# Attention scores: the products with the keys' low parts contract over 64 rows, both halves of the keys side by side in the array

## The chip, the cores and the metric

The kernel runs on one core of a Trainium2 chip. Its time is the device time of one execution in microseconds (us); three runs of the kernel before gave 2217.49, 2220.78 and 2222.54 us, so the time before is their median, 2220.78 us. A difference of 0.2% of that is 4.4 us.

The engines have the names that the profile gives them: PE is the matrix engine (PEld is its load of weights, the operand that stays in the array while the other streams through), DVE the vector engine, ACT the scalar engine, POOL the general engine, SP the one that issues the transfers. PSUM is the memory that matrix products are written to, in banks of 128 rows by 512 floats.

## The reference, cut to what matters

Two layers over 1024 tokens of width 1024. In each layer, one projection of the normalised input feeds three mixers, of which the attention is the one that the change touches:

```python
q = _axial_rope(_rmsnorm(q.reshape(b, s, 8, 64), q_norm_g[l]), tabs)   # 8 query heads of 64
k = _axial_rope(_rmsnorm(k.reshape(b, s, 2, 64), k_norm_g[l]), tabs)   # 2 key heads, 4 query heads each
...
sc = jnp.einsum('bqgrd,bkgd->bgrqk', qblk, k).astype(jnp.float32) * 64 ** -0.5
p = jax.nn.softmax(sc, axis=-1)
return jnp.einsum('bgrqk,bkgd->bqgrd', p, v)
```

A query block has 128 queries, and every query sees all 1024 keys. All arrays are float32. After the mixers come an output projection and a gated convolutional MLP.

## The kernel before, in words

**Numbers in two parts.** The fast matrix product here takes operands of the type `float32r`, which hold fewer digits than float32. To keep the digits, an operand x is split into a high part h (x rounded to `float32r`) and a low part l = x - h, and a product of two split operands is the sum of several matrix products into the same bank. Elsewhere in the kernel a product costs three of them (`mm3`, lines 130 to 132: high by high, high by low, low by high).

**The scores.** A head has 64 channels and the array has 128 rows, so the attention stacks the two parts of the queries: `q_transpose` (line 584) transposes the queries of a block on PE into a bank, ACT copies them, rounded, into rows 0 to 63 of the tile `qT` (line 598), and DVE writes the low parts into rows 64 to 127 (line 599); it does so for the even heads (e = 0) and the odd heads (e = 1) apart. `kv_block` (line 540) writes each key's channels twice, one copy below the other, so that the high parts of the keys lie in all 128 rows, and likewise the low parts. One pass over 128 rows with the keys' high parts then gives (query high + query low) times key high, and a second pass with the keys' low parts gives (query high + query low) times key low. `att_scores` (line 608) makes the scores of 128 queries and one head against 1024 keys in four products, each 128 rows by 512 keys: high and low for the first 512 keys into one bank (lines 616 and 617), then the same for the last 512 keys into the next bank. The keys are in four tiles, one for each key head and half of the keys, in the slots E9, W1, W4 and W5. Each of these groups of four is followed by a maximum over the 1024 scores on DVE (line 619), an exponential on ACT (line 622), a reciprocal on DVE (624) and a scaling on POOL (625).

**The order of the work.** `attention` (line 666) runs units: one unit is a query block and a key head, 16 units in each layer, each with four score groups. A unit has eight steps kc. In step kc, PE transposes the probabilities of the unit before, 128 keys of them (`att_T`, line 633; ACT copies them out at line 637, DVE writes the low parts at line 638), makes a score group of its own unit where kc is 0, 1, 3 or 4, makes some products of the convolution's projections as filler (line 301), and multiplies by the values with a lag of two steps (lines 645 and 646). In step 5 of every second unit `q_transpose` prepares the next query block. PE's order is the order in which this is written, since the stage is under manual order for PE; the other engines' orders are set by a scheduler. Scores go to two pairs of banks (`big`), transposed probabilities to two banks (`pa`), taken in turns.

There are 16 units of four groups in each of two layers, 128 score groups and 512 score products in all.

Of the kernel before, what the change touches and what calls it, by code (L numbers as in the profile page):

```python
# [9 lines left out]
F32R = mybir.dt.float32r  # L10
AF = mybir.ActivationFunctionType
# [3 lines left out]
P = 128  # L15
# [41 lines left out]
class Trunk:  # L57
# [26 lines left out]

    def S(self, tag, shape=(1024,), dt=F32):
        return self.slot(tag, shape, dt)
# [47 lines left out]
    def wpiece(self, src, raw, h, l, eh="p", el="p"):  # L134

        sh = list(src.shape[1:])
        w = self.S(raw, sh)
        self.nc.sync.dma_start(w, src)
        th, tl = self.S(h, sh, F32R), self.S(l, sh, F32R)
        self.split(th, tl, w, eh, el)  # L140
# [3 lines left out]
    def consts(self, L):  # L144
        nc, i = self.nc, self.i
        raw = self.S("W4", [2, P])
        nc.gpsimd.memset(raw, 0.0)
# [37 lines left out]
    def ropetabs(self):  # L185
        nc = self.nc
        cs = self.S("W4", [2, 8, 64])
        nc.sync.dma_start(cs[:, 0], self.i["cos_tab"].rearrange("(b p) c -> p b c", p=P))
# [39 lines left out]
    def spread_g(self, rows, tag):  # L228
# [6 lines left out]
        self.warm(WARM[1])  # L235
        gb = self.S("G6", [KC, P])
        t = self.slot(tag, [D])
# [302 lines left out]
    def kv_block(self, b, hT):  # L540
        nc = self.nc
        if b % 4 == 0:
            for g in range(2):
                self.kT[g][b // 4] = self.S(("E9", "W1", "W4", "W5")[2 * g + b // 4], [2, 512], F32R)
            self.V[b // 4] = self.S(("E3", "E4")[b // 4], [4, 2, 2, 64], F32R)
        acc = self.acc("pa")
        self.tok_mm(acc[:, 0:256], hT, b, self.kvw, 4)
        av = acc[:, 128:256].rearrange("p (g c) -> p g c", c=64)
        V = self.V[b // 4]
        nc.scalar.activation(V[:, b % 4, :, 0, :], av, AF.Copy)  # L550
        nc.vector.tensor_tensor(
            out=V[:, b % 4, :, 1, :], in0=av, in1=V[:, b % 4, :, 0, :].bitcast(F32),
            op=ALU.subtract,
        )
        kr = self.small("kr", [P, 128], bufs=2)
        if b == 0:
            self.ktmp = self.S("E5", [4, 2, 128])
        tmp = self.ktmp[:, b % 4]
        self.rope(kr, acc, 2, self.ktab, b, tmp)
        if b == 0:  # L560
            self.kcat = self.S("E0", [2, 2, 2, 2, 64], F32R)
        kc = self.kcat[:, b % 2]
        k3 = kr.rearrange("p (g c) -> p g c", c=64)
        kb = k3.unsqueeze(2).to_broadcast([P, 2, 2, 64])
        self.split(kc[:, :, 0], kc[:, :, 1], kb, "a", "v")
        pt = self.acc(("po", "pf")[b % 2], dt=F32R)
        kf = kc.rearrange("p g l d c -> p (g l) (d c)")
        for j in range(4):
            nc.tensor.transpose(pt[:, j * P : (j + 1) * P], kf[:, j, :], self.identr)
        for g in range(2):  # L570
            nc.scalar.activation(
                self.kT[g][b // 4][:, :, (b % 4) * P : (b % 4 + 1) * P],
                pt[:, g * 256 : g * 256 + 256].rearrange("p (l t) -> p l t", l=2), AF.Copy,
            )

    def q_block(self, b, hT):
        if b % 2 == 0:
# [5 lines left out]

    def q_transpose(self, b):

        nc = self.nc
        q = self.q[b // 2][:, b % 2, :]
        pt = self.big()[:, 0:512]
        for j in range(4):
            nc.tensor.transpose(  # L590
                pt[:, j * P : (j + 1) * P], q[:, j * P : (j + 1) * P], self.ident
            )
        pv = pt.rearrange("p (j t) -> p j t", j=4)
        qT = self.S("G0", [4, 2, P], F32R)
        for e in range(2):
            src = pv[64 * e : 64 * e + 64]
            h = qT[0:64, :, e, :]
            nc.scalar.activation(h, src, AF.Copy)
            nc.vector.tensor_tensor(
                out=qT[64:128, :, e, :], in0=src, in1=h.bitcast(F32), op=ALU.subtract  # L600
            )
        self.qT = qT.rearrange("p j e t -> p (j e) t")

    def ring(self):
        self.phn += 1
        return f"E{6 + self.phn % 3}"

    def att_scores(self, u, r, pu):

        nc = self.nc  # L610
        g = u % 2
        S = self.big()
        for half in range(2):
            o = S[:, half * 512 : half * 512 + 512]
            q = self.qT[:, 4 * g + r, :]
            nc.tensor.matmul(o, q, self.kT[g][half][:, 0, :], start=True, stop=False)  # L616
            nc.tensor.matmul(o, q, self.kT[g][half][:, 1, :], start=False, stop=True)  # L617
        nm = self.small("nm", [P, 1], bufs=4)
        nc.vector.tensor_reduce(out=nm, in_=S, op=ALU.max, axis=AX.X, negate=True)  # L619
        sm = self.small("sm", [P, 1], bufs=4)  # L620
        p = pu[:, r, :]
        nc.scalar.activation(p, S, AF.Exp, bias=nm, accum_out=sm)  # L622
        rv = self.small("rv", [P, 1], bufs=4)
        nc.vector.reciprocal(rv, sm)  # L624
        nc.gpsimd.tensor_scalar(  # L625
            out=p, in0=p, scalar1=rv, scalar2=1.0, op0=ALU.mult, op1=ALU.mult
        )
# [537 lines left out]
    def run(self, depth):  # L1165
        nc, i = self.nc, self.i
# [5 lines left out]
        for L in range(depth):  # L1172
# [1 line left out]
                self.alloc_x(self.xreg)  # L1174
            self.su, self.vnh, self.vnl = [0, 0], [0, 0], [0, 0]
            self.mB, self.mA = [0, 0], [[0, 0], [0, 0]]
            self.kT, self.V, self.q = [[0, 0], [0, 0]], [0, 0], [0] * 4
            self.phn = self.wun = 0
            if L == 0:
                hT, xs = self.begin(xin)  # L1180
# [189 lines left out]
```

## Time and profile before

| | |
|---|---|
| median of three runs | 2220.78 us (2217.49 to 2222.54) |
| the profiled execution | 2218.71 us, its span 2216.7 us |
| PE busy | 2199.8 us, 99% of the span |
| PEld busy | 1828.3 us, 82% |
| DVE busy | 1505.1 us, 68% |
| ACT busy | 1110.0 us, 50% |
| POOL busy | 1102.5 us, 50% |
| score products | the first starts at 143.8 us, the last at 1456.9 us |
| granted clock of PE | 1.00 |

The attention of the first layer holds the stretch from 155 to 368 us, that of the second the stretch from 1258 to 1471 us.

Times inside the profile count from the first instruction of the profiled execution. In a view by groups, a row gives the line, the engine, the operation, what it writes and reads, the shape, how many there were, their summed and mean durations, and how long the engine had idled just before them. In a timeline a row gives the start and the duration of one instruction, or of several alike that follow each other (the count at the end). A matrix product's row ends later than the next one's row starts, because products are pipelined: what a product costs in a stream is the distance between two starts, not its duration.

### The profile page before, as it was taken

Reading aid. Unit: us, or ns where it says so; the run is one execution under the profiler, and the core shown is the slowest. Engines: PE = TensorE matmul, PEld = TensorE weight load, DVE = VectorE, ACT = ScalarE, POOL = GpSimd, SP = SyncE. Lnnn points to the kernel's source line nnn. Section 1 sums busy time; section 2 is a strip of 40 time slices with the busy share of each in tenths; the row PEclk is TensorE's granted clock in tenths of the full one; section 3 lists DMA queues with packets and bytes.
Section 4 is the critical chain, followed back from the end, with each engine's and each line's share of the span. In section 5 each row is a group of like instructions: output and inputs, shape, how many; then the busy total and the mean of one; then the engine's idle time right before and its main releaser. Section 6 shows DMA issues by size and latency. Waiting matters only on the chain.

```text
span 2216.7 us, 29437 instructions
## 1 busy us (share of the span) xinstructions
PE 2199.8 (99%) x10590; PEld 1828.3 (82%) x10590; DVE 1505.1 (68%) x1973; ACT 1110.0 (50%) x1890; POOL 1102.5 (50%) x1031
## 2 busy tenths in 40 slices
PE   9999999999999999999999999999999999999999
PEld 7888888887888888888888888888788888888887
DVE  6568887177777777754745688862867777777554
ACT  5247776364444444433532477763545444544332
POOL 4364445576767776020133653556667767751100
PEclk9999999999999999999999999999999999999999
DMA  5000002223545453886520000041234545448754
GB/s 178 26 20 10 11 19 96 105 83 98 166 157 168 154 168 123 296 314 216 200 91 11 20 20 1 29 154 47 76 124 152 171 152 167 156 143 326 283 190 164
DMA packets 202020, 281.91 MB, mean 127 GB/s; under 512 B 15598, under 2 KB 121618, under 8 KB 201874
## 3 DMA queue, kind: packets, MB, share of 16 engines
q1 hardware_dynamic: 201874, 280.03, 37.6%
q8 instruction: 83, 1.36, 0.3%
q14 instruction: 63, 0.52, 0.1%
HBM read 199.77 MB, written 80.22 MB: 126 GB/s over the span
## 4 chain that ended last, share of the span: by engine, by line
PE 92%; DVE 2%; POOL 2%; ACT 1%; DMA 1%; issue 1%; SPq 0%; DVEq 0%; POOLq 0%; ACTq 0%
PE pa L890 20%; PE pf L890 9%; PE big L1114 8%; PE pa L1114 5%; PE pa L633 5%; PE pf L301 5%; PE po L890 5%; PE pf L1114 3%; PE po L1114 3%; PE big L616 3%; PE po L645 3%; PE big L617 3%; PE po L646 3%; PE pa L132 2%; PE pa L131 2%; PE pa L130 2%
## 5 line engine op out<-in xcount | busy, mean ns | idle before, releaser
L625 POOL TENSOR_SCALAR H<-H,rv 128x1024 f32<-128x1024 f32 x128 | 144.1, 1127 | 223.3 <-DVE rv L624 223.3
L106 ACT ACTIVATE E<-E 128x512 fp32r<-128x512 f32 (+1 forms) x211 | 133.0, 637 | 162.3 <-POOL E L878 61.0
L638 DVE TENSOR_TENSOR E<-pa,E 128x512 fp32r<-128x512 f32 x256 | 173.5, 688 | 52.2 <-ACT E L637 50.6
L890 PE MATMUL pa<-H,E 128*128 128x512 f32 x840 | 206.6, 390 | 1.4 <-DVE H L936 1.3
L637 ACT ACTIVATE E<-pa 128x512 fp32r<-128x512 f32 x256 | 152.8, 597 | 80.0 <-PE pa L633 78.4
L117 POOL TENSOR_TENSOR E<-E,E 128x512 fp32r<-128x512 f32 x118 | 165.1, 1404 | 50.8 <-ACT E L106 50.8
L890 PEld LDWEIGHTS pa<-H,E 128*128 128x128 f32 x840 | 157.4, 188 | 35.3 <-DVE H L936 2.1
L106 ACT ACTIVATE G<-H 128x1024 fp32r<-128x1024 f32 (+1 forms) x116 | 114.2, 1008 | 142.3 <-PE big L1114 70.8
L117 DVE TENSOR_TENSOR G<-H,G 128x1024 fp32r<-128x1024 f32 (+1 forms) x86 | 99.5, 1160 | 110.8 <-ACT G L106 110.4
L619 DVE TENSOR_REDUCE nm<-big 128x1 f32<-128x1024 f32 x128 | 155.5, 1215 | 8.1 <-PE big L617 8.0
L633 PEld LDWEIGHTS pa<-ident,H 128*128 128x128 f32 x1024 | 127.1, 140 | 35.1 <-DVE E L638 1.6
L633 PE MATMUL pa<-ident,H 128*128 128x128 f32 x1024 | 153.7, 272 | 0.0
L937 ACT ACTIVATE H<-pa 128x512 f32<-128x512 f32 x124 | 73.4, 592 | 156.9 <-PE pa L890 122.6
L622 ACT ACTIVATE H<-big,nm 128x1024 f32<-128x1024 f32 x128 | 142.3, 1112 | 12.4 <-DVE nm L619 12.3
L448 DVE SCALAR_TENSOR_TENSOR big<-H,cst,big 128x1023 f32<-128x1023 f32 x44 | 56.6, 1286 | 99.9 <-ACT big L447 99.9
L117 DVE TENSOR_TENSOR E<-E,E 128x512 fp32r<-128x512 f32 (+1 forms) x94 | 96.1, 1028 | 38.6 <-ACT E L106 38.5
L301 PE MATMUL pf<-H,G 128*128 128x512 f32 x288 | 120.2, 431 | 0.0
L890 PE MATMUL pa<-W,E 128*128 128x512 f32 x340 | 116.0, 390 | 0.6 <-DVE E L117 0.6
L106 ACT ACTIVATE G<-E 128x512 fp32r<-128x512 f32 (+2 forms) x110 | 58.6, 547 | 109.1 <-POOL E L878 29.4
L890 PE MATMUL po<-H,E 128*128 128x512 f32 x408 | 105.4, 390 | 2.0 <-DVE H L936 2.0
L1033 POOL TENSOR_TENSOR E<-E 128x512 f32<-128x512 f32 x26 | 35.3, 1359 | 140.3 <-DMA E<-in_ffn_w_down_dram 140.0
L878 POOL TENSOR_TENSOR E<-E 128x512 f32<-128x512 f32 x66 | 102.5, 1552 | 3.3
(400 smaller groups left out, 6331.5 us busy)
## 6 DMA issues: line engine op xcount, KB each, us to landing
H<-gdram SPq DMA_DIRECT2D x70, 512.0 KB, 6.0
gdram<-H SPq DMA_DIRECT2D x134, 256.0 KB, 2.5
E<-in_ffn_w_up_dram SPq DMA_DIRECT2D x66, 512.0 KB, 4.5
H<-tdram SPq DMA_DIRECT2D x40, 512.0 KB, 5.6
E<-in_w_in_dram SPq DMA_DIRECT2D x30, 512.0 KB, 3.9
H<-in_ffn_w_down_dram SPq DMA_DIRECT2D x30, 512.0 KB, 4.6
out_dram<-H SPq DMA_DIRECT2D x28, 512.0 KB, 2.7
E<-in_ffn_w_down_dram SPq DMA_DIRECT2D x26, 512.0 KB, 6.3
```

What stands on the lines that cost most here:

```text
L106: nc.scalar.activation(out, in_, AF.Copy)
L117: e.tensor_tensor(out=l, in0=src, in1=h.bitcast(F32), op=ALU.subtract)
L301: mm(acc, a[:, k, :], b, start=k + j == 0, stop=k == KC - 1 and j == 2)
L619: nc.vector.tensor_reduce(out=nm, in_=S, op=ALU.max, axis=AX.X, negate=True)
L622: nc.scalar.activation(p, S, AF.Exp, bias=nm, accum_out=sm)
L625: nc.gpsimd.tensor_scalar(out=p, in0=p, scalar1=rv, scalar2=1.0, op0=ALU.mult, op1=ALU.mult)
L633: nc.tensor.transpose(pt[:, r * P : (r + 1) * P], pu[:, r, kc * P : (kc + 1) * P], self.ident)
L637: nc.scalar.activation(hl[:, 0, :], pt, AF.Copy)
L638: nc.vector.tensor_tensor(out=hl[:, 1, :], in0=pt, in1=hl[:, 0, :].bitcast(F32), op=ALU.subtract)
L878: self.nc.gpsimd.tensor_tensor(out=of[t], in0=p, in1=q, op=ALU.subtract)
L890: mm(out, w, x, start=first and k + j == 0, stop=k == 3 and j == 2, skip_group_check=True,)
L1114: nc.tensor.matmul(banks[j], p[:, n, s], r[:, n, :], start=first and n + q == 0 and m < 3, stop=last and n == w - 1 and q == 2, skip_group ...
```

## The change

The products with the keys' high parts stay as they are: 128 rows, queries high and low against the doubled high parts. The products with the keys' low parts now contract over 64 rows only, so that queries low times keys low is left out. The query operand of these is the high part alone. The low parts of the first 512 keys lie in rows 0 to 63 of one new tile `kl`, those of the last 512 keys in rows 64 to 127. For the first half of the keys the query operand is rows 0 to 63 of `qT`; for the second half it is a new tile `q2`, in which ACT writes another copy of the rounded queries to rows 64 to 127, two more copies of 64 rows for each query block. In the program these two products carry a tile of 64 by 128 at row 0 and at row 64 of the array; every other matrix product of both kernels carries 128 by 128. In a group the two products of 128 rows now come first, one for each bank, and the two of 64 rows follow, one for each bank.

```diff
     def kv_block(self, b, hT):
         nc = self.nc
         if b % 4 == 0:
-            for g in range(2):
-                self.kT[g][b // 4] = self.S(("E9", "W1", "W4", "W5")[2 * g + b // 4], [2, 512], F32R)
+            self.kh[b // 4] = self.S(("E9", "W1")[b // 4], [2, 512], F32R)
...
             self.kcat = self.S("E0", [2, 2, 2, 2, 64], F32R)
+
+            self.kl = self.S("W4", [2, 512], F32R)
...
-        for g in range(2):
-            nc.scalar.activation(
-                self.kT[g][b // 4][:, :, (b % 4) * P : (b % 4 + 1) * P],
-                pt[:, g * 256 : g * 256 + 256].rearrange("p (l t) -> p l t", l=2), AF.Copy,
-            )
+        pv = pt.rearrange("p (g l t) -> p g l t", g=2, l=2)
+        t = slice((b % 4) * P, (b % 4 + 1) * P)
+        rows = slice(b // 4 * 64, b // 4 * 64 + 64)
+        nc.scalar.activation(self.kh[b // 4][:, :, t], pv[:, :, 0, :], AF.Copy)
+        nc.scalar.activation(self.kl[rows, :, t], pv[rows, :, 1, :], AF.Copy)
...
     def q_transpose(self, b):
...
         qT = self.S("G0", [4, 2, P], F32R)
+        q2 = self.S("W5", [4, 2, P], F32R)
         for e in range(2):
...
+            nc.scalar.activation(q2[64:128, :, e, :], src, AF.Copy)
         self.qT = qT.rearrange("p j e t -> p (j e) t")
+        self.q2 = q2.rearrange("p j e t -> p (j e) t")
...
         S = self.big()
+        banks = S[:, 0:512], S[:, 512:1024]
         for half in range(2):
-            o = S[:, half * 512 : half * 512 + 512]
-            q = self.qT[:, 4 * g + r, :]
-            nc.tensor.matmul(o, q, self.kT[g][half][:, 0, :], start=True, stop=False)
-            nc.tensor.matmul(o, q, self.kT[g][half][:, 1, :], start=False, stop=True)
+            nc.tensor.matmul(
+                banks[half], self.qT[:, 4 * g + r, :], self.kh[half][:, g, :], start=True, stop=False
+            )
+
+
+        for q, rows, o in ((self.qT, slice(0, 64), banks[0]), (self.q2, slice(64, 128), banks[1])):
+            nc.tensor.matmul(o, q[rows, 4 * g + r, :], self.kl[rows, g, :], start=False, stop=True)
```

On PE, this is the first score group of the second unit in the first layer, before (E9, W1, W4 and W5 hold keys, G0 is `qT`, `pa` and `big` are banks, H0 the probabilities of the unit before):

```order
L633 MATMUL pa_289_1641<-ident_64,H0_262_1526 128x128 x4
L616 MATMUL big_291_1649<-W4_154_742,G0_261_1519 128x512
L617 MATMUL big_291_1649<-W4_154_742,G0_261_1519 128x512
L616 MATMUL big_291_1649<-W5_207_1106,G0_261_1519 128x512
L617 MATMUL big_291_1649<-W5_207_1106,G0_261_1519 128x512
L301 MATMUL pf_299_1668<-H2_3_79,G7_267_1535 128x512
```

and now (W4 is `kl`, W5 is `q2`; the size in these rows is that of the result, which is the same):

```order
L642 MATMUL pa_289_1643<-ident_64,H0_262_1528 128x128 x4
L620 MATMUL big_291_1651<-E9_153_741,G0_260_1518 128x512
L620 MATMUL big_291_1651<-W1_206_1105,G0_260_1518 128x512
L626 MATMUL big_291_1651<-W4_162_787,G0_260_1518 128x512
L626 MATMUL big_291_1651<-W4_162_787,W5_261_1519 128x512
L301 MATMUL pf_299_1670<-H2_3_79,G7_267_1537 128x512
```

There are four products in a group as before, at the same place; the two that read the low parts have moved to its end and follow each other. Nothing else on PE has moved, and the orders of POOL and SP are unchanged.

On ACT, this is the `q_transpose` in the fourth unit of the first layer, before (line 598 writes `qT`, line 637 copies transposed probabilities out, line 622 is the exponential):

```order
L598 ACTIVATE G0_399_2072<-big_398_2067 64x4x128
L622 ACTIVATE H1_365_1947,sm_394_2051<-big_392_2044,nm_393_2049 128x1024
L637 ACTIVATE E8_401_2086<-pa_400_2081 128x512
L598 ACTIVATE G0_399_2072<-big_398_2067 64x4x128
L637 ACTIVATE E6_403_2097<-pa_402_2092 128x512
L637 ACTIVATE E7_406_2112<-pa_405_2107 128x512
```

and now (line 605 writes `q2`):

```order
L601 ACTIVATE G0_400_2077<-big_399_2072 64x4x128
L631 ACTIVATE H1_366_1952,sm_395_2056<-big_393_2049,nm_394_2054 128x1024
L646 ACTIVATE E8_403_2094<-pa_402_2089 128x512
L605 ACTIVATE W5_401_2078<-big_399_2072 64x4x128
L601 ACTIVATE G0_400_2077<-big_399_2072 64x4x128
L646 ACTIVATE E6_405_2105<-pa_404_2100 128x512
L605 ACTIVATE W5_401_2078<-big_399_2072 64x4x128
L646 ACTIVATE E7_408_2120<-pa_407_2115 128x512
```

The write of `q2` for the even heads stands ahead of the write of `qT` for the odd heads and of the copy behind it; that for the odd heads stands ahead of the first copy of the next unit, which is the last row.

More of the change, by code (lines that the diff above doesn't have):

```diff
@@ L1176, in run @@
             self.mB, self.mA = [0, 0], [[0, 0], [0, 0]]
-            self.kT, self.V, self.q = [[0, 0], [0, 0]], [0, 0], [0] * 4
+            self.kh, self.V, self.q = [0, 0], [0, 0], [0] * 4
             self.phn = self.wun = 0
```

## The prediction

> **What bounds the kernel now.** First the page: how much of the span PE is busy, and what the chain of waits consists of.
>
> ```profile
> span 2216.7 us, 29437 instructions
> ...
> PE 2199.8 (99%) x10590; PEld 1828.3 (82%) x10590; DVE 1505.1 (68%) x1973; ACT 1110.0 (50%) x1890; POOL 1102.5 (50%) x1031
> ...
> PE 92%; DVE 2%; POOL 2%; ACT 1%; DMA 1%; issue 1%; SPq 0%; DVEq 0%; POOLq 0%; ACTq 0%
> ```
>
> An average over stages says little about one stage, so the second view is the busy time of each engine in the two attention stretches, and in the stage ahead of the first.
>
> ```profile
> 155.00:368.00 213.00, 212.98 (x1197) 177.51 (x1196) 181.11 (x293) 160.25 (x294) 98.41 (x85) 1.00 0.07 21
> 1258.00:1471.00 213.00, 213.00 (x1197) 177.69 (x1196) 180.93 (x294) 160.84 (x298) 98.81 (x85) 1.00 0.07 21
> ...
> 100.00:140.00 40.00, 40.00 (x241) 35.12 (x240) 20.92 (x68) 10.47 (x28) 21.85 (x29) 1.00 0.05 14
> ```
>
> The columns are PE, PEld, DVE, ACT, POOL. PE never idles in the attention, at full clock; DVE works 85% and ACT 75% of it. So the stage ends when PE has gone through its list, and time leaves it only if the list gets shorter. What does an entry cost? The chain of waits, in order of time, gives each product the distance to the next start:
>
> ```profile
> 201.83 0.44 PE pa L633 x4
> 202.26 0.23 PE big L616
> 202.49 0.23 PE big L617
> 202.72 0.23 PE big L616
> 202.95 0.24 PE big L617
> ```
>
> A product of 512 columns holds the path for 0.23 us, a group of four scores for 0.93, four transposes for 0.44. The timeline of the same place shows the weights beside them:
>
> ```profile
> 201.67 0.60 PE L633 MATMUL pa<-ident,H 128*128 128x128 f32 x4
> ...
> 201.99 0.19 PEld L616 LDWEIGHTS big<-E,G 128*128 128x128 f32 x1
> 202.02 0.47 PE L616 MATMUL big<-E,G 128*128 128x512 f32 x1
> 202.10 0.19 PEld L617 LDWEIGHTS big<-E,G 128*128 128x128 f32 x1
> ...
> 202.33 0.39 PE L617 MATMUL big<-E,G 128*128 128x512 f32 x1
> 202.34 0.19 PEld L616 LDWEIGHTS big<-W,G 128*128 128x128 f32 x1
> ```
>
> Two things are to be seen. In the stream, the load of the next weights (0.19 us) starts with the product before it and is hidden. The first product after the transposes begins only 0.03 after its load, and the next start is 0.31 later rather than 0.23: 0.08 is the price here of weights that could not be loaded ahead.
>
> **The change part by part.** The rows of the low products, over the whole run, and of the copies that write `qT`, over the stretch from 160 to 340 us:
>
> ```profile
> L617 PE MATMUL big<-W,G 128*128 128x512 f32 x192 | 75.7, 395 | 0.0
> ...
> L617 PE MATMUL big<-E,G 128*128 128x512 f32 x64 | 25.0, 391 | 0.0
> ...
> L598 ACT ACTIVATE G<-big 64x512 fp32r<-64x512 f32 x14 | 8.2, 589 | 0.2
> ```
>
> *The low products.* There are 256 of them (192 + 64 at line 617), two in each of 128 groups, and their count doesn't change. If the two of a group, on different rows of the array and into different banks, stream at the same time, the second costs between nothing and 0.08 us (its weights not loaded ahead); if they can't, 0.23. No product of this kernel uses fewer than 128 rows, so no row decides between these. Taking the concurrency, I put the second one at 0.04, halfway, since two loads of 0.19 have to fit ahead of a pair where the stream hides one: 0.23 - 0.04 = 0.19 saved in a group, 128 x 0.19 = 24.3 us. The ends are 128 x 0.23 = 29.4 and nothing. A gain beyond 29.4 is excluded: the products of 128 rows stay, and the first of a pair still has 512 columns to stream.
>
> The Trainium skill (TensorE: Matmul & The Clock Gate, "Part 3: Packing small matmuls") states that products on different row groups run concurrently, starting about 4 ns apart; by that figure, an estimate, the second would cost 0.004 us and the gain would be 28.9 us. No run here shows it yet.
>
> *The changes of shape.* A group goes from 128 rows to 64 and back, 256 changes in all. I take nothing for one: the nearest row is the change from transposes to products and back, and there the chain charges 0.44 and 0.23 with nothing between. The other end is that a product of the new shape can't enter before the last one of the old shape has left: 0.39 from start to end in place of 0.23, that is 0.16 for each change, and 0.19 more if its weights wait too. Below nothing is excluded, as the products before the change keep their 512 columns. This is the widest unknown of the sum, and a rival below.
>
> *The copies for `q2`.* Two ACT instructions of 0.59 us for each of 16 query blocks, 18.9 us of ACT work. What waits behind them, in the fourth unit:
>
> ```profile
> 194.61 0.59 ACT L637 ACTIVATE E<-pa 128x512 fp32r<-128x512 f32 x1
> ...
> 195.22 0.59 ACT L598 ACTIVATE G<-big 64x512 fp32r<-64x512 f32 x1
> ...
> 195.84 0.60 ACT L637 ACTIVATE E<-pa 128x512 fp32r<-128x512 f32 x1
> 195.95 0.69 DVE L599 TENSOR_TENSOR G<-big,G 64x512 fp32r<-64x512 f32 x1
> ...
> 197.34 0.60 ACT L637 ACTIVATE E<-pa 128x512 fp32r<-128x512 f32 x1 [0.90 <-PE pa L633]
> ...
> 198.47 0.39 PE L646 MATMUL po<-E,E 128*128 128x512 f32 x1
> ...
> 199.06 0.48 PE L616 MATMUL big<-E,G 128*128 128x512 f32 x1
> ```
>
> With the first `q2` copy ahead, the odd heads' write of `qT` moves from 195.22 to 195.8, its low parts from 195.95 to 196.6, done at 197.3; the copy of 195.84 moves to 196.4, so that its low parts are done some 0.6 later, at about 197.9, and are read by the product at 198.47 (0.19 earlier in the new kernel, 198.28). The second `q2` copy takes 197.03 to 197.62, in ACT's idle 0.90. The odd heads are first read by the group at 199.06. That even heads are enough for the first group is shown by the start of the stage, where its weights load before the odd heads' low parts are done:
>
> ```profile
> 143.75 0.69 DVE L599 TENSOR_TENSOR G<-big,G 64x512 fp32r<-64x512 f32 x1
> ...
> 143.84 0.19 PEld L616 LDWEIGHTS big<-E,G 128*128 128x128 f32 x1
> ```
>
> So these cost nothing, with 0.3 us to spare; without that cover, 14 blocks x 0.6 = 8 us. ACT's load goes to about (160.25 + 14 x 0.59) / 201 = 84%.
>
> *What is late next.* PE's 213 us become about 201, and DVE's 181 us then fill 90%. In the first half of a unit DVE hardly pauses:
>
> ```profile
> 200.59 0.69 DVE L638 TENSOR_TENSOR E<-pa,E 128x512 fp32r<-128x512 f32 x1
> ...
> 201.20 1.21 DVE L619 TENSOR_REDUCE nm<-big 128x1 f32<-128x1024 f32 x1
> ...
> 202.40 1.28 DVE L638 TENSOR_TENSOR E<-pa,E 128x512 fp32r<-128x512 f32 x2
> ...
> 203.60 1.21 DVE L619 TENSOR_REDUCE nm<-big 128x1 f32<-128x1024 f32 x1
> ```
>
> The bank that the first of these rows empties at 201.28 is written again by the transposes at 201.67; two groups earlier by 0.19 each, they want it at 201.29. With the signal that is a wait of about 0.1 us, once in each of 32 units: 3 us off the gain.
>
> *The keys.* `kv_block` has as many copies as before, one of two over 64 rows. In its stage PE works 40.00 of 40 us and ACT 10.47; nothing changes.
>
> The sum: 24.3 - 3 = 21.3 us off the profiled execution's 2218.71 us, 2197.4; the median of the runs shown lies 2.07 us above that execution, so 2199.5, **2200 us**.
>
> **The rivals.**
>
> *Each change of shape empties the array (slower).* At the third product of a group and at the first product after it, PE waits until the last product has left: 2 x 0.16 - 0.19 = +0.13 us, x 128 = +16.6, 2237 us. It decides from the point where one change costs half of the 0.19 gained, 0.095 us. For it speaks that the end of a product is 0.16 behind the next start, so there is always something to wait for; against it, that between transposes and products nothing is paid. The Trainium skill (TensorEngine Tiling (Array Packing), "Tiling Modes") states this rule: changing the tiling mode, not just the tile, drains the engine. No trace here shows a change of mode. Its chance is 0.22.
>
> *It empties the array, and the weights are loaded only then (slower).* Two loads of 0.19 come on top: 0.13 + 0.38 = +0.51 us, x 128 = +65, 2286 us. For it: a load writes rows of the array whose use is about to change. Against it: the loads run ahead everywhere in the stream. If only the 0.11 between two transposes' starts (0.44 for four) were exposed, it would be +0.35, 2266 us. Chance 0.15.
>
> *Nothing comes of it.* Either the pair doesn't run together (0 saved), or loads are held at the pair's second and at both changes (3 x 0.08 = 0.24 against 0.23). Both give the time before, 2221 us. Chance 0.12.
>
> *DVE's chain becomes the bound (faster, by half).* The wait of 0.1 above grows where the maximum or the exponential also comes late, to 0.4 in each unit, 32 x 0.4 = 13 us: 2221 - 24 + 13 = 2210 us. For it: DVE's near-unbroken rows above. Against it: it idles some 15% now, and the second half of a unit makes no scores. Chance 0.09.
>
> **How the numbers follow.** The forecast has a chance of 0.42. Its own range runs from 2192 (the pair at no cost, 29.4 gained, and no wait at DVE) to 2213 (changes of shape at 0.05 us each). All cases together hold 8 in 10 between 2190 and 2262: this takes in the emptied array, and leaves out the fully exposed weights. About what a measurement of this kernel can tell from no change is 0.2%, 4.4 us. Faster by more: 0.42 + 0.09 = 0.51. Within: 0.12. Slower by more: 0.22 + 0.15 = 0.37.
>
> **What would show it.** In the timeline of a group, the two low products should start within 0.1 us of each other, and the first product after the pair 0.23 to 0.31 after it; then the concurrency and the free change of shape hold. Starts 0.39 apart at the group's third product or behind the pair show the emptied array; a load of weights that begins only where the last product ends shows the second rival; starts of the pair 0.23 apart, the third. Idle of PE released by DVE at the transposes, more than 0.1 us for a unit, would show DVE's chain, and idle released by ACT at a score group the `q2` copies. The forecast is wrong if the score lines together still hold the path for 0.93 us in a group.

## The result and the profile after

The changed kernel takes 2242.36 us (median of four runs, 2241.40 to 2243.51) against 2220.41 us for the kernel before beside it: 1.0098 times as long, 95% interval 1.0086 to 1.0110. It is 22 us slower where 20 us less was forecast. The time lies inside the stated range of 2190 to 2262 us, but on the other side of no change.

The page of the changed kernel, its first lines, and the busy times in its first attention (the columns are PE, PEld, DVE, ACT, POOL):

```profile
span 2240.5 us, 29483 instructions
...
PE 2222.8 (99%) x10590; PEld 1793.9 (80%) x10590; DVE 1503.2 (67%) x1973; ACT 1133.6 (51%) x1922; POOL 1100.2 (49%) x1031
```

```profile
155.00:373.00 218.00, 218.00 (x1165) 157.22 (x1164) 177.63 (x286) 165.60 (x302) 95.38 (x84) 1.00 0.06 18
```

PE has as many products as before, is never idle in the attention and has the full clock. So nothing made it wait from outside: the list itself takes longer. PEld, on the other hand, fell from 83% of this stage (177.51 of 213 us) to 72%. The timeline of one score group shows why (PE and PEld rows):

```profile
204.62 0.40 PE L620 MATMUL big<-W,G 128*128 128x512 f32 x1
...
204.95 0.18 PEld L626 LDWEIGHTS big<-W,G 64*128 64x128 f32 x1 [0.36 <-issue]
204.95 0.49 PE L626 MATMUL big<-W,G 64*128 64x512 f32 x1
204.95 0.18 PEld L626 LDWEIGHTS big<-W,W 64*128 64x128 f32 x1
204.95 0.49 PE L626 MATMUL big<-W,W 64*128 64x512 f32 x1
...
205.37 0.19 PEld L301 LDWEIGHTS pf<-H,G 128*128 128x128 f32 x1 [0.24 <-issue]
205.37 0.50 PE L301 MATMUL pf<-H,G 128*128 128x512 f32 x1
205.48 0.19 PEld L301 LDWEIGHTS pf<-H,W 128*128 128x128 f32 x1
205.72 0.40 PE L301 MATMUL pf<-H,W 128*128 128x512 f32 x1
```

The two low products start at the same time, 204.95: the pair does run side by side. But three distances that were 0.23 are longer now.

| from | to | us | more than 0.23 |
|---|---|---|---|
| last product of 128 rows (204.62) | the pair (204.95) | 0.33 | 0.10 |
| the pair | the first product behind it (205.37) | 0.42 | 0.19 |
| that product | the next (205.72) | 0.35 | 0.12 |

Together 0.41 more, against 0.23 saved by the second low product: +0.18 us in a group, x 128 = 23 us, which is what was measured (22 us). The loads tell which part is what. Before, the load of the next weights started with the product ahead of it. Here the loads of 64 rows start at 204.95, the same moment as their products, 0.33 after the last product of 128 rows, and the load behind the pair starts with its product too. In the waits of PEld this is idle time that nothing outside released ("issue"), twice in nearly every group of the first attention:

```profile
PEld big L626 <- issue: 21.8, 60, 0.4
PEld pf L301 <- issue: 14.1, 58, 0.2
```

### The profile page after: what moved, and what is told of

The parts are those of the page before. It is cut to its first block, busy times and chain, and to the rows that moved or that the text cites. A ratio compares the mean times of both kernels' runs of the same rounds, so it can differ in the third digit from the quotient of the medians.

```text
span 2240.5 us, 29483 instructions
## 1 busy us (share of the span) xinstructions
PE 2222.8 (99%) x10590; PEld 1793.9 (80%) x10590; DVE 1503.2 (67%) x1973; ACT 1133.6 (51%) x1922; POOL 1100.2 (49%) x1031
## 4 chain that ended last, share of the span: by engine, by line
PE 88%; POOL 3%; DMA 3%; DVE 3%; issue 2%; ACT 1%; SPq 0%; POOLq 0%; DVEq 0%; ACTq 0%
PE pa L899 17%; PE pf L899 8%; PE big L1123 8%; PE pf L301 6%; PE pa L1123 5%; PE pa L642 5%; PE po L899 4%; PE pf L1123 3%; PE po L1123 3%; PE big L620 3%; PE po L654 3%; PE po L655 3%; PE big L626 2%; PE pa L130 2%; PE pa L132 2%; PE pa L131 2%
## 5 line engine op out<-in xcount | busy, mean ns | idle before, releaser
L301 PE MATMUL pf<-H,G 128*128 128x512 f32 x288 | 133.9, 478 | 0.0
L106 ACT ACTIVATE G<-E 128x512 fp32r<-128x512 f32 (+2 forms) x110 | 58.6, 547 | 109.6 <-POOL E L887 36.2
```

The source lines that it names most:

```text
L106: nc.scalar.activation(out, in_, AF.Copy)
L301: mm(acc, a[:, k, :], b, start=k + j == 0, stop=k == KC - 1 and j == 2)
```

## The experiments

All times below are medians, each beside the kernel before on the same chip: 2218.89 us for the first four experiments, 2221.01 us for the next four and 2220.37 us for the last. Where a run is compared with the changed kernel, each is taken over its own kernel before (the changed kernel: 22.0 us over). The theory after the result: a change between products of 128 rows and of 64 rows empties the array (about 0.10 us), and only then are the next weights loaded, whose price of about 0.10 us no product hides any more. A round trip of two changes costs 0.41 us. ("Empties" is the theory's word: the rows show when products start, and no run shows the array empty.) Its rivals: products of 64 rows are slow in themselves; or ACT's copies, the new order within the group, or DVE's chain is what cost the 22 us.

### Two round trips in a group

```diff
-        for half in range(2):
-            nc.tensor.matmul(banks[half], qT..., kh[half]..., start=True, stop=False)
-        for q, rows, o in ((qT, 0:64, banks[0]), (q2, 64:128, banks[1])):
+        for half, (q, rows, o) in enumerate(((qT, 0:64, banks[0]), (q2, 64:128, banks[1]))):
+            nc.tensor.matmul(o, qT..., kh[half]..., start=True, stop=False)
             nc.tensor.matmul(o, q[rows]..., kl[rows]..., start=False, stop=True)
```

> The changed kernel with the order of a score group altered: high, low of the first 512 keys, then high, low of the last 512 keys, so that the shape changes four times in a group and the two products of 64 rows never stand side by side. Theory (a change of shape empties the array and its next weights load only then; a round trip of two changes costs 0.41 us, the products of 64 rows are otherwise as fast as those of 128): two round trips and no gain from the pair, 128 x 2 x 0.41 = +105 us on the 2220 of before, about 2325. Rival (products of 64 rows are slow in themselves, 0.23 + 0.41 = 0.64 us for a pair or for one alone, whatever their neighbours are): also 2 x 0.41 on top of four products, 2325; this run does not part these two. Rival (the loss comes from ACT's copies of the queries or from DVE's chain, not from PE): no more than the 22 us lost so far, 2242.

Measured: 2320.39 us, 1.0457 times the kernel before (1.0441 to 1.0472), +101.5 us, or 101.5 / 256 = 0.396 us for each round trip. In PE's timeline every start between shapes is 0.41 to 0.43 behind the one ahead:

```profile
202.25 0.48 PE L621 MATMUL big<-E,G 128*128 128x512 f32 x1
202.66 0.50 PE L622 MATMUL big<-W,G 64*128 64x512 f32 x1
203.09 0.50 PE L621 MATMUL big<-W,G 128*128 128x512 f32 x1
203.52 0.49 PE L622 MATMUL big<-W,W 64*128 64x512 f32 x1
203.94 0.50 PE L301 MATMUL pf<-H,G 128*128 128x512 f32 x1
```

A change costs 0.43 - 0.23 = 0.20 us in either direction. PE is what is slower; the rival of ACT's copies or DVE's chain, with no more than 2242 us, falls.

### One shape for both low products, on the same rows

```diff
-            self.kl = self.S("W4", [2, 512], F32R)
+            self.kl = [self.S(t, [2, 512], F32R) for t in ("W4", "W5")]   # rows 0:64 of each
...
-            nc.scalar.activation(q2[64:128, :, e, :], src, AF.Copy)
...
-        for q, rows, o in ((qT, 0:64, banks[0]), (q2, 64:128, banks[1])):
-            nc.tensor.matmul(o, q[rows]..., kl[rows]..., start=False, stop=True)
+        for half in range(2):
+            nc.tensor.matmul(banks[half], qT[0:64]..., kl[half][0:64]..., start=False, stop=True)
```

> Both low products contract over rows 0 to 63, with the first and the last 512 keys' low parts in two tiles of their own, so that they have one shape but share rows and cannot run side by side; the second copy of the queries (q2) and its ACT instructions are gone. Theory (price per change of shape): one round trip, 0.41 us, and four products of 0.23: 2220 + 128 x 0.41 = 2273 us, and the second low product starts 0.23 us after the first. Rival (slow products of 64 rows): 2 x 0.64 in place of 2 x 0.23: 2220 + 105 = 2325 us, starts of the low products about 0.64 apart. Rival (ACT copies are what was lost): about 2220, since they are gone.

Measured: 2269.83 us, 1.0234 times (1.0217 to 1.0251), +50.9 us: 50.9 / 128 = 0.398 us for the round trip. The timeline, where two products of one line are merged into one row:

```profile
202.48 0.48 PE L617 MATMUL big<-E,G 128*128 128x512 f32 x1
202.79 0.40 PE L617 MATMUL big<-W,G 128*128 128x512 f32 x1
203.12 0.73 PE L623 MATMUL big<-W,G 64*128 64x512 f32 x2
203.78 0.50 PE L301 MATMUL pf<-H,G 128*128 128x512 f32 x1
```

The two low products hold PE for 0.66 us, against 0.42 for the pair of the changed kernel: the second one costs 0.24, as much as a product of 128 rows. The two runs give one price, 0.40 us for a round trip, and the rival of slow products (2325 us here) falls. The changed kernel follows from it: 128 x (0.40 - 0.23) = 21.8 us.

### The pair twice

```diff
+        for q, rows, o in ((qT, 0:64, banks[0]), (q2, 64:128, banks[1])):
+            nc.tensor.matmul(o, q[rows]..., kl[rows]..., start=False, stop=False)
         for q, rows, o in ((qT, 0:64, banks[0]), (q2, 64:128, banks[1])):
             nc.tensor.matmul(o, q[rows]..., kl[rows]..., start=False, stop=True)
```

> The changed kernel with the pair of low products issued twice in each group, so that the low parts are added twice (the output is not the reference's). No change of shape is added. Theory (price per change of shape): the second pair costs one product, 0.23 us: 2242 + 29 = 2272 us, the second pair's start 0.23 after the first's, both of its products at the same time. Rival (slow products of 64 rows): 2242 + 128 x 0.64 = 2324 us.

Measured: 2277.45 us, 58.6 us over the kernel before and so 37 us more than the changed kernel (29 expected, 82 by the rival). The timeline:

```profile
203.74 0.40 PE L620 MATMUL big<-W,G 128*128 128x512 f32 x1
204.06 0.49 PE L626 MATMUL big<-W,G 64*128 64x512 f32 x1
204.07 0.49 PE L626 MATMUL big<-W,W 64*128 64x512 f32 x1
204.17 0.19 PEld L628 LDWEIGHTS big<-W,G 64*128 64x128 f32 x1
204.40 0.39 PE L628 MATMUL big<-W,G 64*128 64x512 f32 x1
204.40 0.39 PE L628 MATMUL big<-W,W 64*128 64x512 f32 x1
204.72 0.50 PE L301 MATMUL pf<-H,G 128*128 128x512 f32 x1
```

Both pairs run side by side. The first pair takes 0.49 from start to end and the second 0.39: the second's loads were done ahead (they start at 204.17), the first's were not. From the second pair to the product behind it is 0.32, where the changed kernel had 0.42 behind its only pair: without the loads, 0.09 remain over 0.23. So the 0.20 of a change is about 0.10 for emptying the array and 0.10 for the loads.

The second pair starts 0.34 behind the first, and that is no price of its own: in the changed kernel the product behind the one at 205.37 starts 0.35 later too, and both follow products that had waited for their loads. Over the whole group the second pair adds 0.34 + 0.32 - 0.42 = 0.24 us, as one product of 128 rows, which is what was expected. PE's busy time says the same, 2253.1 us against 2222.8 in the changed kernel, 30.3 more. The rest of the distance between the two profiled spans (2275.2 less 2240.5, 34.7 us) is idle time of PE, and one wait of this size stands among its waits that the changed kernel has not:

```profile
PE pa L644 <- POOL H L636: 4.4, 4, 1.2
```

DVE's order is another here than in the changed kernel; whether that is why POOL comes late is not shown.

### The pair ahead of the products of 128 rows

```diff
-        (the two products of 128 rows)
-        (the pair)
+        (the pair, start=True)
+        (the two products of 128 rows, stop=True)
```

> The changed kernel with the pair of 64 rows ahead of the two products of 128 rows, so that the first change of shape comes right behind the transposes, whose successor pays for weights not loaded ahead anyway (about 0.08 us in the kernel before). Theory in its form with two parts (the array empties, and the next weights are loaded only then): that part is paid once where it was paid twice, 128 x 0.08 = 10 us less, about 2232. If the price is emptying the array alone: no change, 2242.

Measured: 2240.54 us, 1.0098 times (1.0083 to 1.0113), the same ratio as that of the changed kernel. The 10 us did not come. The timeline:

```profile
201.30 0.60 PE L640 MATMUL pa<-ident,H 128*128 128x128 f32 x4
201.83 0.49 PE L620 MATMUL big<-W,G 64*128 64x512 f32 x1
201.84 0.49 PE L620 MATMUL big<-W,W 64*128 64x512 f32 x1
202.26 0.50 PE L622 MATMUL big<-E,G 128*128 128x512 f32 x1
202.60 0.40 PE L622 MATMUL big<-W,G 128*128 128x512 f32 x1
```

The pair starts 0.53 after the transposes, which hold PE for 0.44: 0.09 for emptying, and then 0.42 to the next product, as behind the pair of the changed kernel. In the kernel before, a product starts 0.35 behind the transposes and its successor 0.31 behind it, 0.66 in all, which is just 0.44 + 0.23: nothing is paid there. The 0.08 us that the prediction read as a price of weights not loaded ahead is only a start that comes early and a second one that comes late. There was no price to merge with.

### The order alone

```diff
-        for half in range(2):
-            (high, low of this half)
+        (high of both halves, then low of both halves, all of 128 rows, in the kernel before)
```

> The kernel before with the changed kernel's order in a group (high, high, low, low), all of 128 rows. Theory: no change of shape, no change of time, 2219. Rival (the order delays the maximum or the weights): up to the 22 us that the change lost.

Measured: 2220.61 us, 0.9998 times the kernel before (0.9988 to 1.0007). The order within the group costs nothing.

### ACT's copies twice

```diff
             nc.scalar.activation(q2[64:128, :, e, :], src, AF.Copy)
+            nc.scalar.activation(q2[64:128, :, e, :], src, AF.Copy)
```

> The changed kernel with each of ACT's copies into q2 issued twice, 32 more instructions of 0.59 us. Theory (the copies are hidden): 2242. Rival (they are on the path): as much again as they cost now; if they were all of the 22 us, 2264; at most 32 x 0.59 = 19 us more.

Measured: 2258.51 us, 37.5 us over the kernel before, 16 us more than the changed kernel. In the changed kernel itself, no wait of PE on these copies stands among the waits; with twice as many the list of PE's waits begins with them:

```profile
PE big L621 <- ACT W L606: 7.9, 16, 1.9
```

So the copies are hidden in the changed kernel, but only just: the second set found no room, with a wait for each of the 16 query blocks. These waits are 7.9 of the 16 us. Behind the longest of them, 1.9 us, the granted clock was 0.68 (the number behind the five engines) from 175 to 180 us, and PE's row has 18 products there where the changed kernel has 27 at 1.00:

```profile
175.00:180.00 5.00, 4.88 (x18) 3.73 (x19) 2.86 (x6) 2.96 (x6) 1.19 (x2) 0.68 0.00 0
```

What else the 16 us hold is not taken apart. That the copies cost the changed kernel nothing is also what the run on the same rows says, which has no such copies: it lies 50.9 - 22.0 = 28.9 us above the changed kernel, and one more product in a group, 128 x 0.23 = 29.4, accounts for that.

### Half as many round trips

```diff
-            (at steps 0, 1, 3, 4: one group, 2 products of 128 rows and a pair)
+            (at steps 0 and 3: two groups, 4 products of 128 rows and then two pairs)
```

> The changed kernel with two score groups made together, at steps 0 and 3 of a unit: four products of 128 rows, then two pairs of 64 rows, so that the round trips are half as many (64). From the runs so far (0.10 to leave, 0.34 from the first pair to the second, 0.32 from there to the next product, 0.11 behind it): a double group holds PE for 0.69 + 0.33 + 0.34 + 0.32 + 0.11 = 1.79 us against 1.85 before, 64 x 0.06 = 4 us less than before, 2215, if the banks are free in time. Rival (the later maximum and exponential now bind, since both banks of scores are emptied behind each other before the next double group): PE waits for the exponential (line 632 or so) at steps 3 and 0, up to 1.5 us for a unit, 32 x 1.5 = 48 us, 2260. The starts within a double group should be those given here in either case.

Measured: 2295.53 us, 1.0336 times (1.0320 to 1.0351). The rival won by more than its estimate. One of the waits of PEld, and those of PE:

```profile
PEld big L628 <- issue: 23.6, 64, 0.7
```

```profile
PE pa L648 <- DVE E L653: 14.9, 42, 0.6
PE big L622 <- ACT W L605: 11.4, 12, 1.2
PE po L660 <- ACT H L637: 8.4, 14, 0.6
PE po L660 <- DVE E L676: 6.0, 9, 0.9
PE pa L648 <- POOL H L640: 6.0, 4, 2.6
```

The changes of shape are indeed half as many (64 at the pairs), and a double group that waits for nothing has the starts that were expected: the first pair 0.33 behind the products of 128 rows, the second 0.34 behind the first, the next product 0.32 behind that (in one of them they start at 213.09, 213.42, 213.76 and 214.08). But PE now waits for DVE's, ACT's and POOL's work behind two groups at once, and for the `q2` copies, the second of which the group at step 1 used to have time for. The five waits shown are 47 us, far more than the 4 us that the sum promised. A kernel that makes all the products and is faster than the one before did not come out of these runs.

### A low product left out, as a pair at no cost would be

```diff
-            (high, low of the first half; high, low of the second half)
+            (high of both halves; low of the first half alone)
```

> The kernel before with the low product of the last 512 keys left out (the output is not the reference's): three products of 128 rows in a group, what a pair side by side at no cost for shapes would come to. Theory: 2219 - 128 x 0.231 = 2189.5, less than 3 us of it lost to DVE as the prediction's step on what is late next has it, 2190 to 2193. Rival (DVE's chain binds): 2219 - 30 + 13 = 2202 or more, with PE idle released by DVE.

Measured: 2238.95 us, 1.0080 times (1.0064 to 1.0097): a fourth of the score products is gone, and the kernel is 18 us slower. The wait is not what the first of the two views below names, as the timeline of one of the 30 shows:

```profile
PE pa L633 <- DVE rv L624: 36.5, 30, 1.3
```

```profile
201.01 1.22 DVE L619 TENSOR_REDUCE nm<-big 128x1 f32<-128x1024 f32 x1
...
202.27 0.69 DVE L638 TENSOR_TENSOR E<-pa,E 128x512 fp32r<-128x512 f32 x1
...
202.88 0.15 DVE L624 RECIPROCAL rv<-sm 128x1 f32<-128x1 f32 x1
...
203.10 0.63 PE L633 MATMUL pa<-ident,H 128*128 128x128 f32 x4 [1.27 <-DVE rv L624]
```

The transposes write the bank that line 638 empties until 202.96; the reciprocal only ended near that time (this is read from the order of the banks, not shown by a row). Line 638 came late because DVE had a maximum (1.22 us) ahead of it. In the kernel before the two stand the other way round at this place (200.59 and 201.20 in the prediction's rows). The scheduler, which is given a shorter list for PE, has put DVE's work into another order. To part the two, a low product (now that of the first half, which no other engine waits for) was taken out after the scheduler had run, so that DVE, ACT and POOL keep their order of before to the instruction:

```diff
+                if half == 0: GONE.append(low)      # low: the product with the first half's low parts
+    (once everything is scheduled: the instructions in GONE are dropped from the program)
```

> The kernel before with one low product of each group (that of the first 512 keys) taken out after the scheduler has run, so that DVE, ACT and POOL keep the order that they have in the kernel before, instruction by instruction (the output is not the reference's). The run that left a low product out ahead of the scheduler took 2239 us, 18 more than before, with PE waiting 36 us, 30 times, for DVE. Theory A (the scheduler's new order on DVE did that; a free pair would have brought its gain): PE idles little, 2220 - 29 = 2191 to 2194 us as the prediction's step on DVE has it. Theory B (DVE's chain has no room whatever the order): PE idles at the transposes about as much as it gained, 2210 to 2240 us.

Measured: 2201.11 us, 0.9912 times (0.9898 to 0.9925), 19.3 us less than the kernel before. The new order was the cause of the slow run. And of the 128 x 0.231 = 29.6 us that PE's list is shorter by, 10 are lost again, at two places (waits of PEld, and the timeline at one of each):

```profile
PEld pa L639 <- DVE E L644: 10.7, 32, 0.4
PEld big L592 <- ACT H L628: 4.6, 11, 0.5
```

```profile
184.15 0.40 PE L652 MATMUL po<-E,E 128*128 128x512 f32 x1
184.44 0.42 PEld L639 LDWEIGHTS pa<-ident,H 128*128 128x128 f32 x4 [0.34 <-DVE E L644]
184.44 0.66 PE L639 MATMUL pa<-ident,H 128*128 128x128 f32 x4
184.86 0.47 PE L618 MATMUL big<-W,G 128*128 128x512 f32 x1
...
188.22 0.39 PE L652 MATMUL po<-E,E 128*128 128x512 f32 x1
188.45 0.60 PE L639 MATMUL pa<-ident,H 128*128 128x128 f32 x4
189.20 0.66 PE L592 MATMUL big<-ident,G 128*128 128x128 f32 x4 [0.15 <-ACT H L628]
```

Lines 639 and 644 of this kernel are the transposes and DVE's low parts; lines 592 and 628 are the transposes of the queries and the exponential. The first place is the one that the prediction named, once in each of 32 units. PEld's idle 0.34 there is not what PE loses: from the product ahead of the transposes to the one behind them it is 0.71 (184.15 to 184.86), where 0.58 to 0.60 is usual and most of these waits make it 0.73, so about 0.14 in a unit, some 4.5 us. At the second place, 11 of the 16 query blocks, the queries' transposes start 0.98 to 1.06 behind the last product where 0.66 is usual, some 4 us more; they write a bank that the exponential has to empty first.

## Why the prediction was wrong, point by point

**What bounds the kernel: right.** PE holds the attention before and after, and what PE's list gained or lost is what the time did.

**The low products: right that they run side by side**, though no row of the kernel before could show it: their starts are 0.00 to 0.01 us apart. The trace agrees with the Trainium skill's page that was cited (TensorE: Matmul & The Clock Gate, "Part 3"), which gives 4 ns. (The rows resolve 0.01 us.) The second one costs nothing in the changed kernel, so the 0.04 taken for the two loads was not needed: in the run with the pair twice the second pair adds 0.24 to a group, as one product does.

**The changes of shape: this is the step that failed.** "I take nothing for one: the nearest row is the change from transposes to products and back." The nearest row was the wrong one. Transposes and products have the same tile, 128 by 128, and changing between them is free; a change of tile costs 0.20 us, from two runs alike (0.396 and 0.398 us for a round trip). With 256 of them the forecast of -24.3 us becomes 128 x (0.40 - 0.23) = +21.8 us.

**The rivals of the emptied array: right in kind, with the sizes of its parts wrong.** The first put 0.16 for leaving and nothing for the loads, 2237 us; the second 0.16 and 0.19, 2286 us. The runs show about 0.10 for leaving and 0.10 for the loads, 2242 us, between the two. The 0.16 was the end of a product's row less the next start; the next shape enters earlier than that end (0.33 behind the start, where the row ends at 0.40). The 0.19 was the whole load; a product starts with its load and ends 0.10 later for it. So the sign that the prediction gave, a start 0.39 behind the last one, did not come either: it is 0.33 at the group's third product and 0.42 behind the pair. The rule of the Trainium skill (TensorEngine Tiling (Array Packing), "Tiling Modes"), that a change of the tiling mode drains the engine, agrees with the trace in that every change costs 0.20 us. The two rivals together had deserved more than a chance of 0.37 against a row that only resembled the case.

**The copies for `q2`: right**, hidden, and with as little room as the 0.3 us of the step says: one more set costs 16 us.

**What is late next: right, but not all of it.** 0.1 us in each of 32 units, 3 us, was the figure; about 0.14, some 4.5 us, is what a list shorter by a product in each group met there. The sum had no term for the transposes of the queries, which lose some 4 us more behind the exponential. So even with the pair and the shapes at no cost at all the time would have been about 2201 us and not 2192 (an estimate, from the run with the order kept).

**The rival that nothing comes of it, and DVE's chain as the bound**, did not decide: the pair runs together, and PE is not idle in the changed kernel.

## What to carry to other kernels

A matrix product on 64 of the array's rows was a change of mode here, not just a smaller product. Count the changes: here one costs 0.20 us, a round trip 0.40, and a pair side by side saves 0.23, so a round trip has to hold at least two pairs before it gains anything (0.06 us with two, which no run here turned into time), and what is gained has to pass the engines behind. When no row of a trace shows an operation, a row that only resembles it is no reason for the cheap end. And a version that leaves work out tests a bound only if the scheduler's order is kept, since the order can move more time than the work.

## What the runs showed that was not expected

Leaving out a product of 0.23 us in each of 128 groups made the kernel 18 us slower, because the scheduler ordered DVE's work anew; with the old order such an omission makes it 19 us faster. The order alone is worth about 37 us here (the two runs leave out different products of the same size).

The second pair of a group starts 0.34 us behind the first, and still costs no more than one product of 128 rows: a start that is late can be followed by one that is early, so a price is read over the whole group and not from one distance.
